# Twelve half steps of an MLP multiplied in plain fp32, and head norms that keep an operand in PSUM

## The chip, the core and the metric

The kernel runs on one core of one Trainium2 chip. The metric is the device time of one execution in microseconds (us). Before the change the median of three executions is 2981.17 us, from 2978.42 to 2985.02. The core's engines run beside each other, each through its own list of instructions in order: TensorE multiplies matrices (PE in the profile, and PEld for loading its stationary operand), VectorE (DVE), ScalarE (ACT) and GpSimd (POOL) work on elements, and SyncE (SP) issues most of the DMA. They wait for one another through semaphores. SBUF is the large on-chip memory that all of them read and write; PSUM is the small one, of eight banks here, to which PE writes its products.

## The reference

One inference step of a diffusion backbone: two layers over 128 context tokens (`x_prompt`) and 1024 latent tokens (`x_sample`), 1024 features wide. All of it is fp32. Cut to what the change touches:

```python
def _rms(x, g):
    return x * lax.rsqrt(jnp.mean(x * x, axis=-1, keepdims=True) + EPS) * g

def _layer(x, mod, lw, ctx):
    sh1, sc1, g1, sh2, sc2, g2 = mod
    h = _rms(x, n1) * (1 + sc1) + sh1
    u_conv, qa, ka, va, qn, kn, vn = jnp.split(h @ w_in, idx, axis=-1)
    a_out = _conv_module(u_conv, ...)          # 31 taps, depthwise
    qa = _rms(qa.reshape(B, L, GQA_HEADS, HEAD_DIM), aqg)   # head norms: mean over 64
    ka = _rms(ka.reshape(B, L, GQA_KV_HEADS, HEAD_DIM), akg)
    qn = _rms(qn.reshape(B, L, NA_HEADS, HEAD_DIM), nqg)
    kn = _rms(kn.reshape(B, L, NA_HEADS, HEAD_DIM), nkg)
    ...
    x = x + g1 * (jnp.concatenate([a_out, b_out, c_out], axis=-1) @ w_out)
    h = _rms(x, n2) * (1 + sc2) + sh2
    x = x + g2 * (jnp.square(jax.nn.relu(h @ w1)) @ w2)     # w1 to 4096, w2 back to 1024
    return x, new_ctx
```

The outputs are both token streams after two layers and the new keys and values of the context.

## The kernel before

**Products in parts.** Most large products are made with three passes. An fp32 operand is split into a high part, which ACT casts to the type fp32r (`acopy`, L96), and a low part, the rest, which DVE subtracts (`tt`, L99). The function `three` then issues high x high, low x high and high x low into the same PSUM bank. A plain fp32 matmul, without such parts, is used where it is small, as for the sums of the layer norms (`psn`, L277).

**A layer** goes through these stages: projection by `w_in` with the convolution beside it, two attentions, output projection, MLP. Both layers run the same code. PE sets the length of most stages; the other work is put between its groups by generators (`pre`, `fill`, `tail`), each advanced by a step at fixed places, so that the order of the instructions of every engine is fixed by the code.

**The projection** (`project`; in the profile 107.1 to 341.6 us for layer 0 and 1586.8 to 1817.8 for layer 1) runs over the columns V0, V1, A0 to A5, VN of 256 and over five groups of tokens (four of 256, one of 128). A group is 48 matmuls of 256 columns into a bank `pst` (24 for the last). `post` then handles the bank. For A0 to A5 it norms the heads. `head_stats` squares on ACT (`sq`), sums over each head of 64 on DVE (`ss`, L420: two, four or eight numbers in each of the 128 partitions), and has ACT work out ss^(-1/2) as exp(-0.5 ln(ss/64 + eps)) (`y`). `head_norm`, a group later, has DVE improve `y` by a Newton step of three tiny operations (`rsq_end`, L102) and multiply the bank by it (`xn`, L99). POOL then applies gains and rotary tables (`o`), and the result is stored to DRAM (`ddA`) and loaded again as `kd`, `qd` for the transposes (`pstr`, L784). The MLP doesn't use these functions. Beside them, in the same stage: the taps of the convolution (`conv_taps`), of which DVE takes most (`cacc`, L102, 1167 columns, three inputs: a tile, a scalar per partition and the sum) and ACT and POOL together the others (`cp` on ACT, `cacc<-cacc,cp` on POOL, L570); the splits of the weights (`wh`, `wl`); and the modulation of the layer, for which PE multiplies loaded weights `aw` (`psmod`, L224), DVE copies the bank (`mt`, L229) and PE transposes it (`psmt`, L233).

All PSUM tiles come in turn from one pool of eight banks (`P`), so a tile gets the bank of the tile taken eight before it and must wait until that one has been read.

**The MLP** uses a scheme of seven products of half-size blocks (P1 to P7) in place of eight. Its second half, `mlp` from L1728 on, walks a list `steps`: q is the half of the inner dimension, p the product, gi the inner block, ns the output blocks. The last 32 entries, the *half steps*, are P5 and P3 for two of the four output blocks at a time, first blocks 0 and 1, then 2 and 3; `early` is the index of the first one. For each step `fetch` loads an input tile `ti` (two blocks in one tile), `ready2` (L1554) splits the input into `ts` and the weights into `w2`, two or more steps ahead, and the loop issues `three` for each output block: 12 matmuls of 128x288 in a half step. The weights lie in the SBUF tiles `HF`, four regions that `w2(b, gi)` addresses. After the last gi of a product, `update` on DVE adds the banks, times the gate `g2`, to the residual `X` (L102).

In layer 0 the generator `tail` runs beside the half steps: it does the norms of the next layer's input (squares on ACT, sums on DVE and POOL, `psn` on PE, then `nx` and `HA` on DVE, ACT and POOL). In the profile these half steps stand from 1453.7 to 1531.1 us. In layer 1 the output is written there instead.

## Time and profile before

One execution was profiled. Its own time was 2982.7 us; the recorded span, from its first to its last instruction, is 2980.9.

| | us |
|---|---|
| median of three executions | 2981.17 |
| lowest, highest | 2978.42, 2985.02 |
| profiled execution, own time | 2982.7 |
| its span | 2980.9 |
| mean granted clock of TensorE | 0.983 of full speed |
| projection of layer 0, layer 1 | 234.5, 231.0 |
| half steps of layer 0 | 77.4 |

The page gives the busy time of every engine, the chain of work that ended last, and groups of like instructions. A row of a group reads: line, engine, operation, output <- inputs with their shapes, count, then busy time in us and mean duration in ns, then the idle time of that engine just before these instructions, with what ended it. A row of the waits reads: the waiting engine, its tile and line, what it waited for, the time in all, the number of waits, and the longest. Two more views are used: the timeline, every instruction of an engine in a stretch of time, and a table of windows, with the busy time of each engine in each stretch.

### The profile page before, as it was taken

To read this page: it belongs to the slowest core of one execution; us is meant where nothing else is said; L and a number is where in the kernel's file an instruction comes from. 1 tells how busy PE (TensorE), PEld (TensorE's weight loads), DVE (VectorE), ACT (ScalarE), POOL (GpSimd) and SP (SyncE) were. 2 spreads that over 40 slices of the span, in tenths; PEclk is the share of its full clock that TensorE was granted. 3 is DMA by queue.
4 is the path that set the end of the run, shared out by engine and by line. 5 is a ranking of instruction groups with operands and counts; after the bars stand their busy time and mean duration, and the time that the engine had idled before them with its cause. 6 is when DMAs were issued, how large, how long until landed. Compare 5 with 4: busy or idle time off the path is not lost.

```text
span 2980.9 us, 52857 instructions
## 1 busy us (share of the span) xinstructions
PE 2844.0 (95%) x20328; PEld 2525.2 (85%) x20328; DVE 2096.1 (70%) x4009; ACT 1401.0 (47%) x2864; POOL 652.5 (22%) x607
## 2 busy tenths in 40 slices
PE   6998999999999999999889989999999999999999
PEld 3878745789999989999868886458999999999999
DVE  6588778764867756768675877788557677585676
ACT  4333356762744443433452353668537444433343
POOL 3576345420000000000224772463100000000000
PEclk8999999999999999999999999999999999999999
DMA  7276302424466678443333672024245666565334
GB/s 286 85 210 167 106 20 61 102 65 139 148 212 198 208 239 300 161 156 96 122 129 106 187 200 75 16 55 111 89 124 179 207 203 196 201 236 183 116 102 161
DMA packets 434876, 444.05 MB, mean 149 GB/s; under 512 B 120512, under 2 KB 308672, under 8 KB 434624
## 3 DMA queue, kind: packets, MB, share of 16 engines
q1 hardware_dynamic: 434624, 440.67, 47.4%
q8 instruction: 160, 2.62, 0.4%
q14 instruction: 92, 0.75, 0.1%
HBM read 307.41 MB, written 133.17 MB: 148 GB/s over the span
## 4 chain that ended last, share of the span: by engine, by line
PE 76%; DVE 13%; ACT 4%; issue 2%; DMA 2%; POOL 2%; SPq 1%; DVEq 0%; POOLq 0%; ACTq 0%
PE ps L1319 23%; PE psb L1319 8%; PE psc L1319 6%; PE pso L1319 5%; PE psa L1319 5%; PE psd L1319 3%; PE psacc L1118 3%; PE pspv L985 2%; DVE cacc L102 2%; PE pspt L969 2%; PE pst L541 2%; PE pst L542 2%; PE pst L543 2%; PE psst L1132 2%; PE psm L1044 2%
## 5 line engine op out<-in xcount | busy, mean ns | idle before, releaser
L1319 PE MATMUL ps<-ts,w2h 128*128 128x288 f32 x3072 | 534.4, 296 | 8.3 <-DVE ts L99 4.8
L1319 PEld LDWEIGHTS ps<-ts,w2h 128*128 128x128 f32 x3072 | 451.7, 189 | 9.3 <-DVE ts L99 5.3
L1319 PE MATMUL ps<-ts,w2l 128*128 128x288 f32 x1536 | 329.2, 295 | 0.1
L96 ACT CAST ts<-ti 128x576 fp32r<-128x576 f32 x256 | 172.1, 672 | 310.2 <-PE ps L1319 208.6
L541 PE MATMUL pst<-wh,HA 128*128 128x256 f32 x1040 | 297.9, 286 | 0.0
L542 PE MATMUL pst<-wl,HA 128*128 128x256 f32 x1040 | 294.3, 283 | 0.2 <-DVE wl L99 0.2
L543 PE MATMUL pst<-wh,HA 128*128 128x256 f32 x1040 | 293.7, 282 | 0.0
L93 ACT ACTIVATE ev<-ev 128x576 f32<-128x576 f32 x240 | 164.7, 686 | 265.1 <-DVE ev L99 261.3
L1319 PEld LDWEIGHTS ps<-ts,w2l 128*128 128x128 f32 x1536 | 247.6, 189 | 0.4 <-DVE w2l L99 0.3
L102 DVE SCALAR_TENSOR_TENSOR X<-ps,mod,X 128x288 f32<-128x288 f32 x336 | 112.2, 410 | 163.5 <-PE ps L1319 163.5
L99 DVE TENSOR_TENSOR ts<-ti,ts 128x576 fp32r<-128x576 f32 x256 | 195.5, 764 | 44.7 <-ACT ts L96 44.7
L541 PEld LDWEIGHTS pst<-wh,HA 128*128 128x128 f32 x1040 | 198.3, 191 | 19.2 <-issue 6.9
L542 PEld LDWEIGHTS pst<-wl,HA 128*128 128x128 f32 x1040 | 198.2, 191 | 0.5 <-DVE wl L99 0.4
L543 PEld LDWEIGHTS pst<-wh,HA 128*128 128x128 f32 x1040 | 198.2, 191 | 0.0
L99 POOL TENSOR_TENSOR nacc<-nacc,nsq 128x512 f32<-128x512 f32 (+1 forms) x12 | 15.8, 1320 | 822.2 <-PE ps L1319 796.3
L1772 POOL COPY yu<-X 128x128 f32<-128x128 f32 x8 | 3.9, 500 | 836.2 <-DVE X L102 824.3
L1319 PE MATMUL pso<-HA,woh 128*128 128x288 f32 x1024 | 177.8, 295 | 0.0
L1046 DVE TENSOR_REDUCE mx<-psm 128x1 f32<-128x384 f32 x288 | 142.3, 547 | 30.1 <-PE psm L1044 30.0
L93 ACT ACTIVATE pt<-psst 128x512 f32<-128x512 f32 x216 | 118.1, 597 | 89.6 <-PE psst L1133 88.7
L99 POOL TENSOR_TENSOR R<-R,pt 128x1024 f32<-128x1024 f32 x60 | 148.3, 2472 | 26.3 <-ACT pt L93 24.3
L1319 PEld LDWEIGHTS pso<-HA,woh 128*128 128x128 f32 x1024 | 149.7, 188 | 0.0
L102 DVE SCALAR_TENSOR_TENSOR cacc<-cin,vecs,cacc 128x1167 f32<-128x1167 f32 x78 | 136.8, 1754 | 11.3 <-POOL cacc L570 10.1
(279 smaller groups left out, 7222.6 us busy)
## 6 DMA issues: line engine op xcount, KB each, us to landing
ti<-hd SPq DMA_DIRECT2D x128, 576.0 KB, 4.0
hd<-ev SPq DMA_DIRECT2D x224, 288.0 KB, 4.2
w1r<-in_mlp_w SPq DMA_DIRECT2D x176, 256.0 KB, 4.0
aw<-in_ada_w SPq DMA_DIRECT2D x160, 256.0 KB, 4.0
HF<-in_mlp_w SPq DMA_DIRECT2D x128, 256.0 KB, 5.3
ddA<-o SPq DMA_DIRECT2D x144, 128.0 KB, 3.0
wr<-in_w_in SPq DMA_DIRECT2D x28, 512.0 KB, 4.1
sd<-ev SPq DMA_DIRECT2D x24, 576.0 KB, 2.8
```

What stands on the lines that cost most here:

```text
L93: nc.scalar.activation(out=out, in_=in_, func=func, scale=scale, bias=bias, **k)
L96: nc.scalar.copy(out, in_)
L99: (eng or nc.vector).tensor_tensor(out=out, in0=a, in1=b, op=op)
L102: nc.vector.scalar_tensor_tensor(out=out, in0=a, scalar=s, in1=b, op0=op0, op1=op1)
L541: mm(o, hi, wh, start=(k == 0), stop=False)
L542: mm(o, hi, wl, start=False, stop=False)
L543: mm(o, lo, wh, start=False, stop=(k == KT - 1))
L969: nc.tensor.transpose(ps[0:n, c], self.p[j][:, o:o + n], ident)
L985: mm(ps[64 * j:64 * j + 64, 0:128], v[j], self.at[j, i], start=(i == 0), stop=(i == nb - 1))
L1046: nc.vector.tensor_reduce(out=mx[j][:, qt, b:b + 1], in_=ps[:, 0:384], op=ALU.max, axis=AX.X)
L1118: mm(acc[64 * j:64 * j + 64, :], v, pt[:, j, :], start=(kt == 0), stop=(kt == 8))
L1319: mm(ps[h][:, 0:HH], x, y[:, h * HH:(h + 1) * HH], start=(start and z == 0), stop=(stop and z == 2), skip_group_check=True)
```

## The change

There are two parts.

**Half steps.** In layer 0 (`not last`), of the first 24 half steps those with an odd gi, twelve in all, are no longer split. `ready2` hands on the weights as they lie in `HF` and the input as it was loaded in `ti`, both plain fp32, and the loop calls `whole`, which issues two plain fp32 matmuls for each output block (four in a half step) where `three` issued six (twelve in a half step).

**Head norms.** `head_stats` takes one more PSUM tile, `pss`, from the pool for every group. ACT works out the last exp twice, once into that tile (`z`) and once into `y` in SBUF. The three tiny operations of the Newton step then read one operand from SBUF and the other from PSUM, and two of them write to PSUM; before, both operands were in SBUF. The SBUF tile `nt` is gone.

```diff
@@ -419,11 +419,18 @@
         y = V([n], "y")
-        rsq_start(ss, y, DH)
-        return x, nt, n, ss, y
-
-    def head_norm(x, nt, n, ss, y):
-        rsq_end(ss, y, V([n], "nt"), DH)
+        small = P("pss")
+        z, t = small[:, 0:n], small[:, 64:64 + n]
+        act(y, ss, ACTF.Ln, scale=1.0 / DH, bias=eps)
+        act(z, y, ACTF.Exp, scale=-0.5)
+        act(y, y, ACTF.Exp, scale=-0.5)
+        return x, nt, n, ss, y, z, t
+
+    def head_norm(x, nt, n, ss, y, z, t):
+
+        stt(t, y, -0.5 / DH, z, ALU.mult, ALU.mult)
+        stt(z, ss, EPS * DH, t, ALU.add, ALU.mult)
+        stt(y, z, 1.5, y, ALU.add, ALU.mult)
         w = x.shape[2]
@@ -1318,6 +1325,11 @@
+    def whole(ps, w, b, start, stop):
+
+        for h in range(2):
+            mm(ps[h][:, 0:HH], w, b[:, h * HH:(h + 1) * HH], start=start, stop=stop, skip_group_check=True)
+
@@ -1556,6 +1568,9 @@
             e = inputs.pop(x)
+            if not last and x >= early and gi % 2 and x < early + 24:
+                weights[x] = w2({"P5": "A21", "P3": "A12"}[p], gi)[:, ns[0] * 128:(ns[-1] + 1) * 128], None, e, None
+                return
             two = S([2, HT], F32R, n="ts")
@@ -1750,7 +1765,10 @@
-                three(chain[n], wh[:, c], wl[:, c], hi, lo, begins, gi == 7 and p in ENDS)
+                if wl is None:
+                    whole(chain[n], wh[:, c], hi, begins, gi == 7 and p in ENDS)
+                else:
+                    three(chain[n], wh[:, c], wl[:, c], hi, lo, begins, gi == 7 and p in ENDS)
```

How the instructions of the engines stand now is shown at three places. The first is DVE in the projection of layer 0, at the fifth and last group of A0 (one token block, so four heads). Before, with all operands but the bank `pst` in SBUF:

```order
L420 TENSOR_REDUCE ss_1287<-sq_1285 128x4
L102 SCALAR_TENSOR_TENSOR cacc_1084<-cin_668,vecs_100,cacc_1084 128x1167 x2
L102 SCALAR_TENSOR_TENSOR nt_1294<-y_1289 128x4
L102 SCALAR_TENSOR_TENSOR nt_1294<-ss_1287,nt_1294 128x4
L102 SCALAR_TENSOR_TENSOR y_1289<-nt_1294,y_1289 128x4
L99 TENSOR_TENSOR xn_1298<-pst_1259,y_1289 128x256
```

And the same place of DVE in the changed kernel, with `pss` the new PSUM tile:

```order
L420 TENSOR_REDUCE ss_1291<-sq_1289 128x4
L102 SCALAR_TENSOR_TENSOR cacc_1087<-cin_668,vecs_100,cacc_1087 128x1167 x2
L102 SCALAR_TENSOR_TENSOR pss_1294<-y_1293,pss_1294 128x4
L102 SCALAR_TENSOR_TENSOR pss_1294<-ss_1291,pss_1294 128x4
L102 SCALAR_TENSOR_TENSOR y_1293<-pss_1294,y_1293 128x4
L99 TENSOR_TENSOR xn_1303<-pst_1263,y_1293 128x256
```

Nothing has moved there: the three tiny operations have the same place behind the taps of the convolution, and other operands. ACT has one instruction more for the group.

The second place is ACT within the half steps of layer 0, around the first `HA` of the next layer's norm. Before, with `ts` and `w` the casts of input and weights of successive half steps:

```order
L93 ACTIVATE rstd_16569<-rstd_16569 128x512
L96 CAST ts_16574<-ti_16474 128x576
L96 CAST w_16576<-HF_83 128x256
L96 CAST ts_16604<-ti_16474 128x576
L96 CAST w_16606<-HF_83 128x256
L96 CAST ts_16634<-ti_16572 128x576
L96 CAST w_16636<-HF_84 128x256
L93 ACTIVATE HA_71<-nx_16652,mod_105 128x512
L93 ACTIVATE nx_16655<-nx_16655,mod_105 128x512
L96 CAST HA_71<-nx_16655 128x512
```

The same stretch of ACT in the changed kernel, from the norm's `rstd` on:

```order
L93 ACTIVATE rstd_16551<-rstd_16551 128x512
L96 CAST ts_16556<-ti_16486 128x576
L96 CAST w_16558<-HF_83 128x256
L96 CAST ts_16602<-ti_16554 128x576
L96 CAST w_16604<-HF_84 128x256
L93 ACTIVATE HA_71<-nx_16620,mod_105 128x512
L93 ACTIVATE nx_16623<-nx_16623,mod_105 128x512
L96 CAST HA_71<-nx_16623 128x512
```

Every other pair of casts is gone, one per tile `ti`, and two pairs stand before the first `HA` where there were three. On DVE the subtractions of the same steps are gone in the same way.

The third place is PE in the half steps, where a split step ends and the first plain one runs, in the changed kernel:

```order
L1326 MATMUL ps_16468<-ts_16327,w_16329 128x288
L1326 MATMUL ps_16469<-ts_16327,w_16329 128x288
L1331 MATMUL ps_16466<-ti_16309,HF_95 128x288
L1331 MATMUL ps_16467<-ti_16309,HF_95 128x288
L1331 MATMUL ps_16468<-ti_16309,HF_95 128x288
L1331 MATMUL ps_16469<-ti_16309,HF_95 128x288
L1326 MATMUL ps_16466<-ts_16359,w_16361 128x288
```

Where twelve matmuls from `ts` and `w` stood, four stand that read the loaded tiles themselves. Over the program PE has 96 rows fewer, DVE 24 fewer, and ACT 36 more: 24 casts less and 60 exps more.

## The prediction

> **What bounds the kernel now.** I read the page first, for the engine that fills the span, and then only the two stages that the change touches.

> ```profile
> PE 2844.0 (95%) x20328; PEld 2525.2 (85%) x20328; DVE 2096.1 (70%) x4009; ACT 1401.0 (47%) x2864; POOL 652.5 (22%) x607
> PE 76%; DVE 13%; ACT 4%; issue 2%; DMA 2%; POOL 2%; SPq 1%; DVEq 0%; POOLq 0%; ACTq 0%
> ```

> TensorE is busy for 95% of the span and holds 76% of the chain that ended last. So an edit on VectorE (DVE) or ScalarE (ACT) pays only where PE stands still for those engines, at most the idle time that the trace shows there, and an edit that gives PE more to do costs that in full. The table of three windows (columns: window, length, busy time and count of PE, PEld, DVE, ACT, POOL, granted clock, DMA share, GB/s) shows the projection of layer 0, the half steps at the end of its MLP, and the projection of layer 1:

> ```profile
> 107.10:341.60 234.50, 219.81 (x1731) 198.12 (x1729) 175.50 (x238) 80.03 (x163) 148.46 (x118) 0.97 0.62 170
> 1453.70:1531.10 77.40, 60.87 (x389) 56.27 (x388) 57.66 (x100) 43.24 (x87) 21.84 (x12) 0.93 0.48 152
> 1586.80:1817.80 231.00, 218.04 (x1734) 195.35 (x1735) 177.78 (x239) 80.87 (x164) 149.29 (x118) 0.99 0.61 168
> ```

> The half steps are the weak stage: PE idles 16.5 of 77.4 us there. The projections lose 14.7 and 13.0 us of PE in 231 to 235. Who PE waited for, first in the half steps, then in the two projections (us in total, times, longest):

> ```profile
> PE ps L1319 <- ACT w L96: 6.4, 3, 2.4
> PE ps L1319 <- DVE ts L99: 3.6, 4, 1.9
> PE ps L1319 <- DVE X L102: 3.5, 2, 2.0
> PE ps L1319 <- DVE w L99: 2.9, 2, 2.0
> ```

> ```profile
> PE psmod L224 <- DMA aw<-in_ada_w: 5.9, 5, 1.7
> PE psmt L233 <- DVE mt L229: 5.7, 1, 5.7
> PE pstr L784 <- DMA kd<-ddA: 3.1, 1, 3.1
> ```

> ```profile
> PE psmt L233 <- DVE mt L229: 5.5, 1, 5.5
> PE psmod L224 <- DMA aw<-in_ada_w: 4.8, 4, 1.7
> PE pstr L784 <- DMA kd<-ddA: 2.4, 1, 2.4
> ```

> In the half steps 12.9 of the 16.4 us waited for are the high and low parts (ts and w), which is just what the change thins out. In the projections PE stands once for a late DVE copy (mt) and at the end for k, which passes DVE, POOL and a store on its way; five or four waits are for the loads aw.

> **Part A: twelve half steps without high and low parts.** The groups of the half-step window:

> ```profile
> L1319 PE MATMUL ps<-ts,w 128*128 128x288 f32 x384 | 60.5, 316 | 16.5 <-ACT w L96 6.4 <-DVE ts L99 3.6 <-DVE X L102 3.5
> L99 DVE TENSOR_TENSOR ts<-ti,ts 128x576 fp32r<-128x576 f32 x27 | 23.0, 852 | 15.7 <-ACT ts L96 15.7
> L99 DVE TENSOR_TENSOR w<-HF,w 128x256 fp32r<-128x256 f32 x27 | 14.5, 538 | 0.0
> L96 ACT CAST ts<-ti 128x576 fp32r<-128x576 f32 x26 | 17.4, 668 | 17.2 <-PE ps L1319 11.8 <-POOL wl L99 3.5 <-DVE ts L99 1.0
> L96 ACT CAST w<-HF 128x256 fp32r<-128x256 f32 x26 | 10.4, 401 | 0.0
> ```

> Taken away from DVE: 12 x (0.852 + 0.538) = 16.7 us, which leaves 57.7 - 16.7 = 41.0. From ACT: 12 x (0.668 + 0.401) = 12.8, leaving 30.4. On PE, 12 steps x 12 = 144 matmuls go and 12 x 4 = 48 plain fp32 ones come. The price of one of each, from the timeline of PE (start, length, count):

> ```profile
> 1454.81 8.63 PE L1319 MATMUL ps<-ts,w 128*128 128x288 f32 x64
> 1463.34 1.13 PE L277 MATMUL psn<-nacc,ones 128*128 128x512 f32 x2
> ...
> 734.38 1.19 PE L277 MATMUL psn<-nacc,ones 128*128 128x512 f32 x4
> 735.37 0.38 PE L1319 MATMUL pso<-HA,woh 128*128 128x288 f32 x1
> ```

> 64 of the old ones from 1454.81 to 1463.34 are 0.133 us each. The norm's psn product is plain fp32 already: it leaves two records for each matmul, and its four records for 512 + 64 columns take 735.37 - 734.38 = 0.99 us; half as many columns, 288, take 0.495. So PE pays 48 x 0.495 = 23.8 for 144 x 0.133 = 19.2, **+4.6 us**. Its floor in the stage goes from 384 x 0.133 = 51.2 to 55.8, above what is left on DVE and ACT: the stage changes its bound from the splits to PE.

> What it loses above the floor is 77.4 - 51.2 = 26.2 now: 16.4 in the waits above and 9.8 that no wait names (restarts after them, and a granted clock of 0.93 where the projections have 0.97 and 0.99). Afterwards I keep the 3.5 for X (the residual update must empty the chain's banks, and no part of it is removed) and three tenths of the other 12.9, 3.9, since the next layer's norm chain runs on the same DVE and ACT queues between the splits; and the unnamed 9.8 in proportion, x 7.4 / 16.4 = 4.4. Stage: 55.8 + 3.5 + 3.9 + 4.4 = 67.6, **-9.8 us**. Bounds: all the loss but X goes, 55.8 + 3.5 = 59.3, -18.1; none goes, +4.6. The three tenths is a choice. What hides the remaining splits is the previous step's PE time: a pair of steps, one plain (1.98 us) and one split (1.60), gives DVE 3.6 us for 1.4 us of splits, where it had 3.2 for 2.8.

> **Part B: head norms with an operand in PSUM.** Both layers run 30 of these norms each. The rows of the tiny DVE operations, those of four and eight columns (twelve of two columns are left out), two that read PSUM already, and the ACT Exp that the change doubles:

> ```profile
> L102 DVE SCALAR_TENSOR_TENSOR nt<-y 128x4 f32<-128x4 f32 x24 | 23.0, 960 | 6.0 <-ACT y L93 6.0
> L102 DVE SCALAR_TENSOR_TENSOR nt<-y 128x8 f32<-128x8 f32 x32 | 15.9, 497 | 6.1 <-ACT y L93 6.1
> L102 DVE SCALAR_TENSOR_TENSOR nt<-ss,nt 128x8 f32<-128x8 f32 x32 | 13.3, 415 | 1.1
> L102 DVE SCALAR_TENSOR_TENSOR y<-nt,y 128x8 f32<-128x8 f32 x32 | 12.0, 375 | 1.1
> L102 DVE SCALAR_TENSOR_TENSOR y<-nt,y 128x4 f32<-128x4 f32 x24 | 9.6, 401 | 0.8
> L102 DVE SCALAR_TENSOR_TENSOR nt<-ss,nt 128x4 f32<-128x4 f32 x24 | 7.2, 298 | 0.8
> L99 DVE TENSOR_TENSOR mod<-psmt,vecs 128x16 f32<-128x16 f32 x12 | 1.5, 165 | 0.8 <-PE psmt L233 0.8
> L99 DVE TENSOR_TENSOR xn<-pst,y 128x128 f32<-128x128 f32 x4 | 1.2, 291 | 0.7 <-DVE y L102 0.4
> L93 ACT ACTIVATE y<-y 128x8 f32<-128x8 f32 x32 | 6.7, 209 | 1.0
> ```

> 168 operations take 81.0 us, 482 ns each, though they touch eight numbers a partition. The means hide two kinds, as the timeline shows (DVE, then POOL):

> ```profile
> 230.59 0.15 DVE L102 SCALAR_TENSOR_TENSOR nt<-y 128x8 f32<-128x8 f32 x1
> 230.78 2.71 DVE L102 SCALAR_TENSOR_TENSOR nt<-ss,nt 128x8 f32<-128x8 f32 x1
> 235.02 5.84 DVE L102 SCALAR_TENSOR_TENSOR cacc<-cin,vecs,cacc 128x1167 f32<-128x1167 f32 x2
> 245.07 1.42 DVE L102 SCALAR_TENSOR_TENSOR cacc<-cin,vecs,cacc 128x1167 f32<-128x1167 f32 x1
> ...
> 230.77 2.70 POOL L570 TENSOR_TENSOR cacc<-cacc,cp 128x1167 f32<-128x1167 f32 x1 [1.32 <-ACT cp L93]
> ```

> One of them takes 0.15, the next 2.71, and it ends with the POOL instruction that began beside it. So some wait out a POOL instruction. The price with an operand in PSUM lies between 165 ns (mod<-psmt,vecs, one SBUF and one PSUM input) and 291 (xn<-pst,y with sixteen times as many columns). I take 165, the row nearest in size. At most 81.0 - 168 x 0.165 = 53 us of DVE go, 27 a layer.

> [...]

> That row is why I don't book 27: two cacc steps take 5.84 where one takes 1.42, so 3.0 of it is the same wait. A tiny operation that no longer waits hands part of the POOL instruction on to the next cacc step, so I count half of the 27 as DVE time won, some 13 a layer, over 30 groups. PE's gain is smaller still: mt comes 5.7 and 5.5 us late, at about the middle of the stage, where half of the 13 (6.6) has been won: I take 5.0 in each layer, and leave a remainder. The kd wait ends in a chain that goes on past DVE into POOL and a store, so I take 1.0 of 3.1 and 1.0 of 2.4. The loads aw don't hang on DVE: nothing. **B: 2 x (-5.0 - 1.0) = -12.0 us.** Bounds: nothing at all, or all of these waits in both layers, 14.7 + 12.7 = -27.4.

> Added work: 60 more ACT Exp at the 0.209 of the row; ACT is busy 80 of 234.5 us in the stage, which hides 30 x 0.2 = 6 us. If DVE stood waiting for y every time it would lose these 6 us a layer; the idle of 6.0 and 6.1 in both layers says that it seldom does. And one more of the eight PSUM banks per group, below.

> [...]

> **Sum.** -9.8 - 12.0 = -21.8. The profiled execution took 2982.7 by its own time (span 2980.9 and 1.8 around it), 1.5 above the median 2981.17. 2982.7 - 21.8 = 2960.9, less 1.5 is **2959.5 us**.

> **Rivals.** Each time is against the median.
> - *The wait only moves on* (chance 0.14). Every POOL instruction is waited out by the next cacc step instead, so mt stays late and B gives 2: 2981.2 - 9.8 - 2 = 2969. For it: the 5.84 row. [...]
> - *The half steps stay bound by the norm chain* (0.10). The splits were only the last to come; A gives 0 with the +4.6 inside: 2981.2 - 12 = 2969. For it: DVE X and the norm's work in the same queues. Against: 41 us of DVE in 56 of PE.
> - *Both* (0.06): 2979, not to be told from no change.
> - *More* (0.09): A near its bound (-16) and the DVE lead reaching kd and aw as well (-20): 2945.
> - *Slower: the bank* (0.05). With pss taking banks in turn, a group's pst gets the bank of the pst four groups earlier, not seven or eight, so PE waits if DVE's xn is late. The tightest place, DVE's xn of the fourth group before, and PE's start:

> ```profile
> 1735.75 0.42 DVE L99 TENSOR_TENSOR xn<-pst,y 128x256 f32<-128x256 f32 x1
> ...
> 1742.07 0.39 PE L541 MATMUL pst<-wh,HA 128*128 128x256 f32 x1
> ```

> 1742.07 - 1736.17 = 5.9 us of slack. It decides once DVE is later than that there, after about 64 of a layer's 84 tiny operations. At a mean of 750 ns, 268 above now: 64 x 0.268 - 5.9 = 11.3 us a layer, 2981.2 - 9.8 + 22.5 = 2994; A is eaten from a mean of 650 on. Against: that is over twice the 291 row.

> **How the numbers follow.** The forecast (A -4 to -16, B -5 to -18: 2947 to 2972) has 0.56; with the rest they make 1. The range 2944 to 2973 takes in forecast, both 2969 cases and most of *more*; out of it are *both*, *slower*, and the tails, some 0.18. About 0.2%, 6 us, is what a measurement of this kernel can tell from no change. Faster by more than that (below 2975): 0.56 + 0.14 + 0.10 + 0.09 = 0.89, less 0.02 for tails: 0.87. Within: 0.06 + 0.02 = 0.08. Slower: 0.05.

> **What would show it.** In the profile after: tiny pss and y operations at 0.16 to 0.3 us with no 2.7 us ones, and longer cacc steps instead; PE's wait for mt under 1 us; the half-step stage at 64 to 72 us, its plain matmuls as two records 0.24 us apart, and DVE X first among its waits. The prediction is wrong if the pss operations still wait for POOL, if pst waits for DVE xn, or if the PE time of a plain matmul isn't 0.5 us.

## The result and the profile after

The changed kernel takes 2960.9 us (median of four, 2957.46 to 2962.24); the kernel before, run beside it, 2983.1. The ratio is 0.9925, with a 95% interval of 0.9907 to 0.9942: some 22 us faster, where 21.7 were forecast (2981.2 to 2959.5) and the range was 2944 to 2973. A second measurement of the same kernel, among the experiments, gave 0.9907 (0.9891 to 0.9924). The total is right. Its parts are not: the half steps gave less than was forecast and the head norms much more, and the two errors cancel.

First the page of the changed kernel, busy times and the chain that ended last:

```profile
span 2958.6 us, 52764 instructions
PE 2840.7 (96%) x20280; PEld 2515.8 (85%) x20280; DVE 2025.6 (68%) x3985; ACT 1403.0 (47%) x2900; POOL 649.2 (22%) x607
PE 80%; DVE 10%; ACT 3%; issue 3%; DMA 2%; POOL 2%; SPq 0%; DVEq 0%; POOLq 0%; ACTq 0%
```

VectorE is 70.5 us less busy, and its share of the chain has gone from 13% to 10%; TensorE's busy time has hardly moved (-3.3). (PE counts 48 records fewer, though 96 instructions are gone, since each of the 48 plain matmuls leaves two records.) So the gain is mostly time in which TensorE stood. The same three windows as before, the two projections and the half steps:

```profile
107.50:329.30 221.80, 215.52 (x1730) 193.57 (x1729) 147.91 (x238) 86.18 (x193) 150.64 (x118) 1.00 0.66 180
1440.90:1511.00 70.10, 62.63 (x341) 53.22 (x340) 44.25 (x80) 32.51 (x64) 17.41 (x11) 0.95 0.52 166
1565.40:1793.30 227.90, 218.38 (x1731) 196.21 (x1729) 150.40 (x239) 86.95 (x194) 148.44 (x118) 0.99 0.63 170
```

Layer 0's projection went from 234.5 to 221.8, the half steps from 77.4 to 70.1, layer 1's projection only from 231.0 to 227.9. In the first of them the granted clock rose from 0.97 to 1.00. DVE's busy time fell by 27.6 and 27.4 us in the two projections, by 13.4 in the half steps.

What happened to the tiny operations, in the groups by shape (DVE):

```profile
L102 DVE SCALAR_TENSOR_TENSOR cacc<-cin,vecs,cacc 128x1167 f32<-128x1167 f32 x78 | 142.4, 1826 | 18.5 <-POOL cacc L577 17.3
L99 DVE TENSOR_TENSOR wl<-wr,wh 128x1024 fp32r<-128x1024 f32 x33 | 60.2, 1824 | 31.8 <-ACT wh L96 25.5 <-issue 4.6 <-DMA aw<-in_ada_w 0.9
L102 DVE SCALAR_TENSOR_TENSOR pss<-ss,pss 128x8 f32<-128x8 f32 x32 | 5.5, 170 | 1.1
L102 DVE SCALAR_TENSOR_TENSOR y<-pss,y 128x8 f32<-128x8 f32 x32 | 5.3, 166 | 1.1
L102 DVE SCALAR_TENSOR_TENSOR pss<-y,pss 128x8 f32<-128x8 f32 x32 | 5.2, 164 | 8.2 <-ACT y L93 8.2
L102 DVE SCALAR_TENSOR_TENSOR pss<-ss,pss 128x4 f32<-128x4 f32 x24 | 4.0, 166 | 0.8
L102 DVE SCALAR_TENSOR_TENSOR y<-pss,y 128x4 f32<-128x4 f32 x24 | 3.9, 161 | 0.8
L102 DVE SCALAR_TENSOR_TENSOR pss<-y,pss 128x4 f32<-128x4 f32 x24 | 3.9, 160 | 8.1 <-ACT y L93 8.1
```

The 168 operations that took 81.0 us take 27.8, all of one kind, with means of 160 to 170 ns. The wait for `y` in front of them has grown from 12.1 to 16.3 us, 75 ns for each of the 56 groups shown: that is the second Exp on ACT (`b_bank`, below, has that Exp without the new operands, and the same 16.3). Three rows of the kernel before belong beside these:

```profile
L102 DVE SCALAR_TENSOR_TENSOR cacc<-cin,vecs,cacc 128x1167 f32<-128x1167 f32 x78 | 136.8, 1754 | 11.3 <-POOL cacc L570 10.1
L99 DVE TENSOR_TENSOR wl<-wr,wh 128x1024 fp32r<-128x1024 f32 x33 | 53.3, 1616 | 28.4 <-ACT wh L96 22.1 <-issue 4.6 <-DMA dx<-X 1.5
L102 DVE SCALAR_TENSOR_TENSOR y<-nt,y 128x2 f32<-128x2 f32 x4 | 10.5, 2614 | 0.1
```

Two larger operations with two SBUF inputs took on some of what the tiny ones lost: the convolution's `cacc` (5.6 us more) and `wl`, the low part of the weights (6.9 us more). And the twelve tiny operations of two columns, which the forecast left out, were not small: they took 14.9 us before, 10.5 of it in the row shown, and take 1.9. All 180 together went from 95.9 to 29.7 us.

The waits of PE in the half steps, and in layer 1's projection:

```profile
PE ps L1326 <- DVE ts L99: 2.5, 3, 1.4
PE ps L1326 <- DVE X L102: 2.3, 1, 2.3
PE ps L1326 <- ACT w L96: 1.4, 2, 1.1
PE ps L1326 <- DVE w L99: 0.8, 1, 0.8
```

```profile
PE pstr L791 <- DMA kd<-ddA: 4.5, 1, 4.5
PE psmod L224 <- DMA aw<-in_ada_w: 4.0, 4, 1.3
...
PE psmt L233 <- DVE mt L229: 1.0, 1, 1.0
```

In layer 1 the mt wait fell from 5.5 to 1.0 as forecast, but the kd wait grew from 2.4 to 4.5, where a fall to 1.4 had been forecast. That, and the clock in layer 0, had to be explained.

### The profile page after: what moved, and what is told of

Read it like the earlier page. It is cut to its first block, busy times and chain, and to the rows that moved or that the text cites. A ratio compares the mean times of both kernels' runs of the same rounds, so it can differ in the third digit from the quotient of the medians.

```text
span 2958.6 us, 52764 instructions
## 1 busy us (share of the span) xinstructions
PE 2840.7 (96%) x20280; PEld 2515.8 (85%) x20280; DVE 2025.6 (68%) x3985; ACT 1403.0 (47%) x2900; POOL 649.2 (22%) x607
## 4 chain that ended last, share of the span: by engine, by line
PE 80%; DVE 10%; ACT 3%; issue 3%; DMA 2%; POOL 2%; SPq 0%; DVEq 0%; POOLq 0%; ACTq 0%
PE ps L1326 23%; PE psb L1326 7%; PE psc L1326 6%; PE pso L1326 5%; PE psa L1326 5%; PE pst L548 3%; PE pst L549 3%; PE pst L550 3%; PE psd L1326 3%; PE psacc L1125 3%; PE pspv L992 2%; PE pspt L976 2%; PE psmod L224 2%; PE psst L1139 2%; PE psm L1051 1%
## 5 line engine op out<-in xcount | busy, mean ns | idle before, releaser
L96 ACT CAST ts<-ti 128x576 fp32r<-128x576 f32 x244 | 164.1, 672 | 310.8 <-PE ps L1326 212.4
L93 ACT ACTIVATE ev<-ev 128x576 f32<-128x576 f32 x240 | 164.7, 686 | 264.2 <-DVE ev L99 260.4
L99 DVE TENSOR_TENSOR ts<-ti,ts 128x576 fp32r<-128x576 f32 x244 | 187.9, 770 | 54.9 <-ACT ts L96 54.8
L102 DVE SCALAR_TENSOR_TENSOR X<-ps,mod,X 128x288 f32<-128x288 f32 x336 | 112.2, 409 | 162.2 <-PE ps L1326 162.1
L548 PEld LDWEIGHTS pst<-wh,HA 128*128 128x128 f32 x1040 | 197.0, 189 | 19.2 <-PE pst L550 5.2
L99 POOL TENSOR_TENSOR nacc<-nacc,nsq 128x512 f32<-128x512 f32 (+1 forms) x12 | 12.8, 1070 | 815.8 <-PE ps L1326 789.7
L93 ACT ACTIVATE pt<-psst 128x512 f32<-128x512 f32 x216 | 118.0, 596 | 94.2 <-PE psst L1140 93.2
L102 DVE SCALAR_TENSOR_TENSOR cacc<-cin,vecs,cacc 128x1167 f32<-128x1167 f32 x78 | 142.4, 1826 | 18.5 <-POOL cacc L577 17.3
L99 POOL TENSOR_TENSOR R<-R,pt 128x1024 f32<-128x1024 f32 x60 | 147.1, 2452 | 31.5 <-ACT pt L93 29.4
```

Source lines behind the costliest of these rows:

```text
L93: nc.scalar.activation(out=out, in_=in_, func=func, scale=scale, bias=bias, **k)
L96: nc.scalar.copy(out, in_)
L99: (eng or nc.vector).tensor_tensor(out=out, in0=a, in1=b, op=op)
L102: nc.vector.scalar_tensor_tensor(out=out, in0=a, scalar=s, in1=b, op0=op0, op1=op1)
L548: mm(o, hi, wh, start=(k == 0), stop=False)
```

## The experiments

The table gives for each kernel the length of the stages in its one profile (us; a projection from the start of its first matmul to that of its last, the half steps to the start of the next stage), and the ratio to the kernel before with its 95% interval.

| kernel | projection 0 | half steps | projection 1 | ratio |
|---|---|---|---|---|
| before | 234.4 | 77.3 | 230.8 | 1 |
| changed | 221.8 | 70.1 | 227.9 | 0.9925 (0.9907 to 0.9942) |
| changed, again (`whole_again`) | 222.1 | 69.5 | 223.6 | 0.9907 (0.9891 to 0.9924) |
| part A alone (`a_only`) | 233.0 | 69.9 | 233.1 | 0.9982 (0.9973 to 0.9991) |
| part B alone (`b_only`) | 221.4 | 79.0 | 220.1 | 0.9930 (0.9917 to 0.9943) |
| B's bank alone (`b_bank`) | 232.1 | 77.3 | 230.6 | 1.0008 (0.9997 to 1.0020) |
| no POOL additions (`no_pool`) | 219.9 | 77.7 | 220.1 | 0.9904 (0.9871 to 0.9938) |
| three passes, no split (`a_nosplit`) | 234.6 | 66.9 | 230.9 | 0.9971 (0.9955 to 0.9988) |
| split and plain (`a_dead`) | 233.3 | 80.3 | 231.4 | 1.0001 (0.9986 to 1.0017) |
| psmt later (`mt_later`) | 234.6 | 77.4 | 233.1 | 1.0016 (1.0006 to 1.0025) |
| changed, k later (`ab_kd`) | 220.3 | 70.0 | 220.6 | 0.9892 (0.9880 to 0.9905) |
| B alone, k later (`b_kd`) | 222.1 | 77.6 | 219.3 | 0.9924 (0.9908 to 0.9940) |
| k later, 24 plain (`ab_kd_all`) | 219.6 | 62.0 | 221.2 | 0.9893 (0.9874 to 0.9911) |

Stages that none of these edits touches scatter between profiles too: layer 1's attention took 307.1 to 312.8 us. So a stage is read to some 3 us, and only where several profiles agree. The half steps scatter less: 77.3 to 79.0 us in the six kernels with the half steps of before, 69.5 to 70.1 in the four with part A.

**The parts alone.** `a_only` has the half steps of the change and the head norms of before, `b_only` the reverse.

> Part A alone: the twelve plain half steps, head norms as before. My theory: the half-step stage alone changes, from 77.4 us to about 70 (as it is in the profile of the whole change), both projections keep their wait for mt of 5 to 6 us and their kd wait, and the time falls by 7 to 10 us against the kernel before. Rival (the gain comes from the head norms and the granted clock alone): no change within 3 us. Rival (the stage is bound by the norm chain): stage at 76 us or more, time -1 or worse.

> Part B alone: head norms with an operand in PSUM, all half steps split. My theory by the forecast: -12 us, the half-step stage unchanged at 77 us, mt waits under 1.5 us in both layers. What the profile of the whole change adds: layer 0's projection alone shrinks by some 12 us, 8 of it named waits and 4 a clock that no longer falls after the two long stops of TensorE, layer 1's by only 3 because its kd wait grows. If that is the cause, layer 0's projection is again near 222 us and layer 1's near 228 here, and the time falls by 12 to 16. Rival (the wait only moves on to cacc): projections at 231 to 235, time -2.

A alone gives 0.18%, 5 us; B alone 0.70%, 21 us. So neither part is without effect, the norm chain doesn't bind the half steps (69.9, not 76), and B's wait doesn't only move on (221.4 and 220.1, not 231 to 235). The half steps move with A and only with A, the projections with B and only with B. What the two waits of layer 0 became in B alone:

```profile
PE psmod L224 <- DMA aw<-in_ada_w: 5.9, 5, 2.3
PE pstr L791 <- DMA kd<-ddA: 0.7, 1, 0.7
```

No wait for mt is left, and 2.4 of 3.1 us of the kd wait went. Named waits fell from 14.7 to 6.6 us; the stage fell by 13.0. In the other five PE was busy before: for the same matmuls its busy time fell from 219.8 to 214.8 us, which is the granted clock, shown below. In layer 1 B alone wins 10.7, 8.0 of it in named waits (12.7 before, 4.7 here), and the kd wait there is 1.2 us: the 4.5 of the changed kernel isn't a property of B.

**What the tiny operations waited for.** `no_pool` is the kernel before without GpSimd's additions of the convolution:

```diff
                 act(p, cin[:, k:k + CW], ACTF.Copy, scale=dww(L.l, j, k))
-                nc.gpsimd.tensor_tensor(out=acc[:, 0:CW], in0=acc[:, 0:CW], in1=p, op=ALU.add)
```

> The kernel before, with GpSimd's additions of the convolution (cacc<-cacc,cp, 42 of 2.7 us) left out, so that the convolution lacks those taps. My theory (a tiny operation with two SBUF operands waits for a GpSimd instruction that is running): the mean of the tiny operations falls from 482 ns to under 280, no one longer than 2.3 us (what is left is GpSimd's gains and rotary products), cacc on VectorE falls to near 1.45 us, the waits for mt go in both layers, and the projections are near 221 us. Rival (the tiny operations are long by themselves, by a semaphore or a write that isn't seen yet): their mean stays above 400 ns.

The source view of L102 in layer 0's projection of that kernel (count: shortest/median/longest in ns, first and last start):

```profile
L102 DVE SCALAR_TENSOR_TENSOR cacc<-cin,vecs,cacc x39: 1417/1434/3394, 133.7 to 344.9; 128x1167 f32<-128x1167 f32 x39
L102 DVE SCALAR_TENSOR_TENSOR nt<-y x30: 149/163/1256, 120.7 to 295.2; 128x8 f32<-128x8 f32 x16, 128x4 f32<-128x4 f32 x12, 128x2 f32<-128x2 f32 x2
L102 DVE SCALAR_TENSOR_TENSOR nt<-ss,nt x30: 160/166/649, 120.9 to 295.4; 128x8 f32<-128x8 f32 x16, 128x4 f32<-128x4 f32 x12, 128x2 f32<-128x2 f32 x2
L102 DVE SCALAR_TENSOR_TENSOR y<-nt,y x30: 161/166/378, 121.1 to 295.6; 128x8 f32<-128x8 f32 x16, 128x4 f32<-128x4 f32 x12, 128x2 f32<-128x2 f32 x2
```

The same operations with all operands in SBUF are short once the long POOL instructions are gone; none exceeds 1.26 us, where 2.7 had been common, and the mean of all 180 in both layers is 215 ns. Both projections come to 220 us, as with B. A miss: `cacc` was expected near 1.45 us and its mean is 1.63 (127.3 us for 78); POOL's gains and rotary products, which are left, are what it can still wait for. That the tiny operations are long by themselves is out.

**The bank.** `b_bank` takes `pss` and writes the second Exp into it, but keeps the operands in SBUF:

```diff
+        small = P("pss")
+        z = small[:, 0:n]
         act(y, ss, ACTF.Ln, scale=1.0 / DH, bias=eps)
+        act(z, y, ACTF.Exp, scale=-0.5)
         act(y, y, ACTF.Exp, scale=-0.5)
...
         rsq_end(ss, y, V([n], "nt"), DH)
```

> Half of part B: the bank pss is taken and ACT writes its second Exp into it, but the three tiny operations read SBUF tiles as before (nothing reads pss). My theory: no gain and no loss beyond 2 us; tiny operations still at about 500 ns mean with 2.7 us ones, mt waits of 5 to 6 us; TensorE still doesn't wait for xn at a pst. Rival (the slower case of the forecast: a bank taken more is itself dear): pst waits for xn and the time grows by 5 us or more. Rival (the gain of B is a matter of banks or of order, not of operands): the time falls like that of part B.

The ratio is 1.0008 and its interval takes in 1. The 168 tiny operations take 79.1 us, 471 ns each, against 81.0 and 482. No `pst` waits for `xn` in the profile, though the mt waits are 4.0 and 3.9 us where 5 to 6 were expected. The slower rival of the prediction (the bank) doesn't occur, and the gain of B is in the operands.

**Whose lateness it is.** `mt_later` leaves DVE's tiny operations as before and lets PE come for `mt` later. The two empty steps also move back what the generator does next, on PE and on DVE alike: DVE's sum `mod`, and its memset of the next `psmod` with PE's products behind it.

```diff
             nc.vector.tensor_copy(mt, ps)
             yield
+            if not first:
+                yield
+                yield
```

> The kernel before, without either part; only TensorE's transposes psmt come two filler steps (two to four groups) after the copy mt that they wait for. VectorE's tiny operations keep their waits for GpSimd. Theory 1 (what B gains is TensorE's stops in the projection, for mt above all, and the granted clock that falls behind them): mt's waits of 5.7 and 5.5 us go, the clock doesn't fall there, layer 0's projection comes to 225 to 227 us and layer 1's to 225, and the time falls by 9 to 16 us. Theory 2 (VectorE's lateness is what matters, the stop only moves on): kd's waits grow from 3.1 and 2.4 us to 7 or more, and the time falls by less than 6 us.

PE's waits in layer 0's projection of that kernel:

```profile
PE psmod L224 <- DVE psmod L219: 15.9, 1, 15.9
PE psmod L224 <- DMA aw<-in_ada_w: 4.1, 5, 1.6
```

The mt wait is gone, and one stop of 15.9 us for the next thing that DVE owes, the memset of `psmod`, has come. In layer 1 there are 4.2 for the same memset and 8.2 for `wl`. The kernel is no faster (1.0016). The second theory holds in its main point, though not with kd as the next wait: where DVE runs behind PE, it stops PE at whatever PE needs first. B removes lateness, not one wait.

**What the half steps pay.** In `a_nosplit` the twelve steps make no parts of their own but multiply in three passes by the parts of the step before, so those products are left out (the line that keeps `parts` isn't shown); in `a_dead` all steps split, and twelve multiply plainly and leave the parts unused.

```diff
             if not last and x >= early and gi % 2 and x < early + 24:
-                weights[x] = w2({"P5": "A21", "P3": "A12"}[p], gi)[:, ns[0] * 128:(ns[-1] + 1) * 128], None, e, None
+                weights[x] = parts[0]
                 return
```

```diff
             weights[x] = wh, wl, hi, lo
+            if not last and x >= early and gi % 2 and x < early + 24:
+                weights[x] = src, None, e, None
```

> Head norms as before. The twelve half steps make no high and low parts of their own, but three passes are kept: they multiply by the parts of the step before (so these twelve products are not the reference's). VectorE and ScalarE are relieved as in part A, TensorE keeps its 144 matmuls. In part A alone the stage took 69.9 us. By the forecast's term (a plain step costs 0.38 us more than a split one, 4.6 for twelve), the stage falls to 65 us. By the timeline of the changed kernel (plain 1.73 a step, but the split step after it 1.79 for 1.58, so 0.33 a pair) it falls to 66. Rival (the plain products cost TensorE nothing that shows): 70 us as in part A.

> Head norms as before. All half steps make their high and low parts, but the same twelve as in part A multiply the plain operands and leave those parts unused. VectorE and ScalarE work as before, TensorE as in part A. My theory (the splits bind the stage): nothing of the 7.4 us gained, stage at 77 to 81 us. Rival (the gain is not the splits but fewer matmuls, or fewer waits of TensorE since it needs parts for half of its steps only): 70 to 73 us.

Without splits and with the old matmuls the stage takes 66.9 us, 3.0 less than part A; with splits and the plain matmuls 80.3, 3.0 more than before. Both say the same of PE's price, some 3 us of the 4.6 forecast, and both that DVE and ACT bound the stage: taking 144 matmuls for 48 gains nothing while the splits stay. The whole windows, `a_dead` and then `a_nosplit`:

```profile
1450.60:1530.90 80.30, 65.61 (x340) 55.27 (x339) 57.48 (x100) 43.35 (x87) 21.79 (x12) 0.91 0.46 146
```

```profile
1450.30:1517.20 66.90, 58.63 (x388) 54.83 (x388) 46.12 (x80) 32.51 (x64) 17.73 (x11) 0.95 0.47 151
```

The second is 13.4 us shorter, and 7.0 us less of it is PE's busy time; DVE has 46.12 us of work there, against 57.48 in the first.

**The kd wait of layer 1.** `ab_kd` is the whole change with the transposes of k a group later, `b_kd` the same without A:

```diff
         load_q(0)
         yield
+        yield
         for b in kb:
             yield from k_build(b, True)
```

> The whole change, and the transposes of k moved one group later in both projections (one more empty step after the loads of kd and qd are issued). My theory: in layer 1 the kd wait of 4.5 us goes, and with it the fall of the granted clock that follows it (0.72 over 12 us, 3.4 us of TensorE work), so layer 1's projection falls from 228 to 220 to 223 us, layer 0's stays within 2 us of 222, and the time falls by 3 to 8 us against the whole change (about -27 against before). Rival (the wait is paid anyway, by the later work of the attention that starts a group later): layer 1's attention stage grows by as much, and the time is that of the whole change.

> Part B with the transposes of k one group later, all half steps split. Part B alone has kd waits of 0.7 and 1.2 us, the whole change 4.5 in layer 1, the whole change with the later transposes none. My theory (A's 7 us is there, but in the whole change the longer kd wait and the clock after it take it back): this kernel gains 1 to 4 us over part B alone (0.7 + 1.2 and at most some clock), 2958 to 2961 where part B alone has 2962 and the whole change with the later transposes 2950; the difference of this one to the latter is A, 6 to 9 us. Rival (A is worth nothing beside B): this kernel is at 2950 too.

> The changed kernel once more, for a second profile of it. If the kd wait of 4.5 us in layer 1 belongs to its order and not to one execution, it is there again at 3 to 6 us, with a fall of the granted clock behind it, and layer 1's projection is again some 7 us longer than in part B alone (220.1); time 2957 to 2963. If it was one execution's, the wait is under 2 us and the projection near 220.

`ab_kd` loses the kd wait, layer 1's projection comes to 220.6 and the attention behind it stays at 309.2: the rival, that it is paid later, is out. Its 0.9892 lies below both measurements of the changed kernel, 0.9925 and 0.9907; the interval is clear of the first's and overlaps the second's, so the 3 to 8 us expected are borne out only roughly. `b_kd` is at 0.9924, less than 2 us from B alone, at the low end of what was expected; so A is worth 0.3% beside it, near the 7 us by which it shortens its stage. That a longer kd wait belongs to the order of the whole change, as the expectation of `b_kd` had it, is not what the second run of the changed kernel showed. There PE waits 1.7 us at that place, with no fall of the clock behind it; projection 1 is 223.6, and the time is 2953.36. (The view names ACT's `y` for these 1.7 us, but the load of kd had landed only 0.1 us before that `y`, so the kd wait is shorter there, not gone.) The two profiles differ in the load of kd. First the changed kernel, then its second run, SyncE's issue and the time from issue to landing:

```profile
L144 SPq DMA_DIRECT2D kd<-ddA x2: 562/1358/2153, 1734.1 to 1737.8; - x2
...
DMA to landing us min/median/max: 5.5/6.2/6.9
```

```profile
L144 SPq DMA_DIRECT2D kd<-ddA x2: 562/564/565, 1733.8 to 1735.8; - x2
...
DMA to landing us min/median/max: 4.9/5.2/5.4
```

In the first profile the first of the two issues took 2.15 us instead of 0.56, and its load landed 6.9 us after its start instead of 4.9. PE was ready for these transposes at 1736.7 and began them at 1741.2; in the second it was ready at 1737.1 and began them at 1738.8. The same issue took 1.1 us in the profile of B alone. So the load leaves PE no margin, and the execution decides how long PE stops. Why the issue was slow that time wasn't found.

**More plain steps.** `ab_kd_all` is `ab_kd` with the condition on `gi % 2` left out: all of the first 24 half steps are plain.

> The whole change with the later transposes of k, and all 24 of the first half steps plain, not twelve (no high and low parts in them). A plain step took 1.73 us, a split one behind it 1.79. My theory: nothing is left of the splits on the way, so the stage is 24 x 1.73 + 8 x 1.6 = 54.3 and the two waits for X of 2 to 3 us, 57 to 62 us where the whole change has 70.1; time 2938 to 2945. Rival (the norm chain or the loads of ti bind instead): stage at 66 us or more, time within 4 us of 2950.

The stage falls to 62.0 us, the upper end of what was expected. Its window shows PE busy for 60.73 of these 62.00 us, at a clock of 1.00:

```profile
1436.20:1498.20 62.00, 60.73 (x292) 49.49 (x291) 37.08 (x62) 25.29 (x48) 17.65 (x11) 1.00 0.45 143
```

It also gives the price of a plain product undisturbed, in the timeline of PE:

```profile
1436.19 11.80 PE L1332 MATMUL ps<-ti,HF 128*128 128x288 f32 x48
1447.83 1.02 PE L277 MATMUL psn<-nacc,ones 128*128 128x512 f32 x2
```

48 records in 11.64 us are 0.2425 each, 0.485 a matmul. The 1.73 us a step on which the expectation was built was read from starts between unlike neighbours, and was too short; 24 x 1.94 + 8 x 1.6 = 59.4 and 1.2 for the one wait left come nearer. By time it is 0.9893 (2946.44 us), which can't be told from `ab_kd` (2949.76); the 8 us show in the stage alone. Both are the fastest kernels of this study; against the second measurement of the changed kernel their intervals still overlap.

## Why the prediction came out, point by point

- **PE's price of a plain step, +4.6.** Right in size: 48 x 0.485 for 144 x 0.133 is +4.1, and the two experiments on it gave 3.0 and 3.0 with what waits absorb.
- **The half steps, -9.8.** The mechanism is right, the size too large: -7.2, and -7.4 in part A alone; by time A is worth 5. The named waits were 7.4 by the forecast and are 7.0 (2.5 + 2.3 + 1.4 + 0.8); those for X fell, those for splits stayed a little higher, so X was not first among them as forecast (2.3, behind 2.5 for `ts`). The term that failed is the unnamed loss, which I let shrink in proportion to the waits, from 9.8 to 4.4. The floor after is 240 x 0.133 + 48 x 0.485 = 55.2, so it is 70.1 - 55.2 - 7.0 = 7.9. Part of it is the clock, 0.95 in the window.
- **The tiny operations, 53 us of DVE at most.** Exact for the 168 that the sum counts: 81.0 - 27.8 = 53.2 us. As a bound on the part it was too low, since the twelve of two columns that it left out gave another 13.0. The value taken, 165 ns, is what they have, and the upper bound of 291 was far off. With two SBUF inputs the operations took up to 2.71 us in the projections of the kernel before, and at most 1.26 in layer 0's where the long POOL instructions are left out (`no_pool`); with one SBUF input, in the changed kernel, they take 0.15 to 0.17 us in both projections, with those POOL instructions in place. The operand from PSUM made them no longer: means of 160 to 170 ns against medians of 163 to 166 with SBUF operands in `no_pool`.
- **"I count half of the 27 as DVE time won."** This step failed. DVE's busy time in the projections fell by 27.6 and 27.4 us, the whole 27 a layer. The tiny operations lost 66 us with those of two columns, and of these some 12 came back inside larger operations with two SBUF inputs: 6.9 in `wl`, which the forecast didn't name, and 142.4 - 136.8 = 5.6 in `cacc` (in B alone 9.0 and 1.2). That is less than a fifth, not half. `cacc` also waits 7.2 us longer ahead of it, for POOL's sum; that is DVE that had caught up, and no wait of PE in the projections is for `cacc`.
- **PE's gain of 6.0 a layer.** Too small by about half: 13.0 and 10.7 in part B alone. mt (-5.0 a layer) was right: 5.7 and 4.5 to 5.5 went. The kd wait fell by 2.4 and 1.2 instead of 1.0. What was missing altogether is a term for the clock: behind the mt and kd stops of layer 0 PE ran at half speed, 5.0 us of its busy time, and behind the mt stop of layer 1 for 2.8 us, by estimate 1.4 of it.
- **Sum.** -21.8 against 22 and 28 us in two measurements. A was some 2.5 us too large in its stage (5 by time), B some 9 too small by time (21 for 12); in the first profile a kd wait took a part of B back. The number was met by luck: errors of both signs met.
- **The rivals.** That the wait only moves on is shown wrong by B alone, the norm chain by A alone, the bank by `b_bank`. *More* had 0.09, and its picture, DVE's lead reaching kd, is nearer to what B did than the forecast was.

## What to carry to other kernels

Read the mean of a tiny operation against its shortest instance: 482 ns beside 150 is a wait inside the instruction, and no wait view names it. A wait in front of TensorE is a symptom where the engine that owes it runs late as a whole: `mt_later` moved the stop and gained nothing, B took the lateness out and gained 21 us. And a stop of TensorE is booked at its length plus the slow clock behind it, which here was 0 to 3 us more.

## What the runs showed of the hardware

**The clock behind a stop.** In the kernel before PE stood for 5.72 us until 242.87, for mt. The windows around it, two us each, with the granted clock third from the end:

```profile
238.00:240.00 2.00, 0.00 (x0) 0.00 (x0) 2.00 (x1) 0.27 (x1) 1.63 (x1) 1.00 0.64 136
240.00:242.00 2.00, 0.00 (x0) 0.00 (x0) 1.84 (x5) 0.00 (x0) 0.00 (x0) 0.55 0.00 0
242.00:244.00 2.00, 1.13 (x6) 1.16 (x7) 2.00 (x3) 0.00 (x0) 1.27 (x1) 0.50 0.00 0
244.00:246.00 2.00, 2.00 (x11) 2.00 (x11) 2.00 (x3) 0.78 (x3) 0.00 (x0) 0.50 0.79 169
246.00:248.00 2.00, 2.00 (x15) 2.00 (x15) 1.84 (x7) 1.16 (x2) 1.03 (x1) 0.74 0.43 94
248.00:250.00 2.00, 2.00 (x20) 2.00 (x19) 2.00 (x2) 1.67 (x3) 2.00 (x2) 1.00 0.05 12
```

PE does 11 matmuls in a window of 2 us where it does 20 later: from 242.87 to 247.04 it runs at half rate, which costs two us more than the stop. The same was behind the kd stop of layer 0 before (3.1 us; a clock of 0.72 in the 12 us from 288) and that of layer 1 after:

```profile
1736.00:1748.00 12.00, 7.55 (x44) 7.37 (x44) 1.34 (x5) 4.75 (x9) 6.01 (x4) 0.72 0.97 262
1748.00:1760.00 12.00, 12.00 (x102) 10.90 (x100) 5.38 (x13) 6.75 (x15) 4.39 (x2) 1.00 0.77 223
```

**Two kinds of fp32 product.** The plain one costs 0.485 us for 128x288, three passes of fp32r 0.40. On TensorE it is a fifth dearer; but a half step then needs none of the 1.39 us of DVE and 1.07 of ACT that its parts took, and where those two bound the stage, as here, it wins: 69.9 us for 77.3 in part A alone.
